# Hybrid encoder trunk: feature-major inputs, the first norm applied behind the projections, and the relative-bias rows copied in DRAM

## Chip, cores and metric

One core of one Trainium2 chip (trn2). The metric is the device time of one execution in microseconds (us), lower is better; a kernel's time is the median of its runs.

## The reference

A trunk of two layers over 272 tokens (16 meta tokens ahead of 256) with 1024 features, all in float32. In each layer an RMS norm, one input projection for four mixers in parallel (SSD, GLA, windowed attention "SWA", full attention "GQA"), one output projection, then a norm and a feed-forward block: SwiGLU in layer 0, eight experts with top 2 in layer 1.

```python
def _rmsnorm(x, w):
    xf = x * lax.rsqrt(jnp.mean(jnp.square(x), axis=-1, keepdims=True) + EPS)
    return xf * w

h = jnp.concatenate([meta, x], axis=1)
for i in range(2):
    u = _rmsnorm(h, norm_mix_w[i])
    (z, xbc, dt_raw, gq, gk, gv, gr, ga, sq, sk, sv, aq, ak, av) = jnp.split(u @ w_in[i], offs, axis=-1)
    y_ssd = _ssd_mixer(z, xbc, dt_raw, ...)
    y_gla = _gla_mixer(gq, gk, gv, gr, ga, ...)
    y_swa = _swa_mixer(sq, sk, sv, swa_sink[i], rel_bias)   # scores + rel_bias[bucket(key - query)]
    y_g2 = _gqa2d_mixer(aq, ak, av, ...)
    h = h + jnp.concatenate([y_ssd, y_gla, y_swa, y_g2], axis=-1) @ w_out[i]
    h = h + (_swiglu, _moe)[i](_rmsnorm(h, norm_ffn_w[i]), ...)
return _rmsnorm(h, final_norm_w)[:, 16:]
```

The bias of the windowed attention depends on key minus query alone: 543 distances times 4 heads, the same in both layers.

## The kernel before

The residual `hT` and the normed input `uT` lie feature-major: [128 features, 8 chunks, 272 tokens]. A float32 product is made of three float32r products (`mm3`, `proj_mm`): every operand is held as a high part, which ScalarE (ACT) casts (L144), and a low part, which VectorE (DVE), or for some tiles GpSimd (POOL), subtracts (L145). So each 1 MB weight tile `w` that SP loads (L140) gives two pairs of `wx` tiles of 128x1024. The pool `wa` has three buffers for the loaded tiles; a load waits in SP's queue until the splits of an earlier tile are done. SP issues in order: a load that waits holds all behind it. TensorE (PE) runs the products. Each engine's order is set ahead by the scheduler, which simulates a timeline from the program's order and a few hints (`high_priority`, `issue_after`).

**First norm.** `x` comes token-major. ACT squares it with row sums (L249 to L251), `rsx` becomes the inverse root, 24 transposes on PE give `hT` (L277), and 24 products with the diagonal matrices `dg` of the factors (in `normed`, L256 to L272) give the normed, transposed chunks `xn`, which ACT and DVE split into `uTh` and `uTl`. In layer 0 the projections thus need no factor: `evac` (L441) copies on ACT. In layer 1, `uT` comes without the factors, and `evac` multiplies by `rsB`, the factors on every partition, on DVE.

**Parameters.** 118 rows of parameters arrive by a dozen small loads and are transposed into the columns `colsP` (L294); others come through POOL's queue (L284 to L290).

**Projections of layer 0**, in PE's order: `dtga` (SSD steps and GLA gates), `gq`, `gk`, `gv`, the six `xbc` blocks of SSD, then those of the attentions, `z` and the gates, between mixer work.

**The relative bias** (`late_setup`, L298 to L334) is set up once, after GLA's front. `fb` [4 heads, 543] is the product of `rel_bias` with a one-hot matrix. It is written to DRAM 128 times per head, and read back skewed, with a row pitch one shorter than the row, so that partition q sees the distances of query q:

```python
scr = dr.tile([4, 128, RELW], F32, name='scr')
SP.dma_start(scr, fb[:, None, :].to_broadcast([4, 128, RELW]))
SP.dma_start(bias[j], bass.AP(tensor=scr.tensor, offset=scr.offset + o,
                              ap=[[RELW - 1, 128], [128 * RELW, 4], [1, L]]))
V.tensor_tensor(bias[j], bias[j], msk[:, j:j + 1, :].to_broadcast([128, 4, L]), op=ALU.add)
```

`bias` serves the windowed attention alone, whose scores come after SSD's and the full attention's first work. The SSD tiles spoken of below: `e` (L640, L699), masked decays times scores of the meta keys, and `y` (L118), its product with `x`.

Of the kernel before, what the change touches and what calls it, by code (L numbers as in the profile page):

```python
# [33 lines left out]
RELW = 543  # L34


def _consts():
# [30 lines left out]
    put('selP', np.arange(8)[:, None] % 4 == (p // 32)[None])  # L68
# [25 lines left out]
    ds = np.zeros((128, 256))  # L94
    for j in range(2):
        ds[:4, 128 * j:128 * j + 128] = 2 * j + (p // 64)[None] == np.arange(4)[:, None]
    masks = np.concatenate(m + [ds], axis=1).astype(np.float32)
# [13 lines left out]
def build(tc, A, out, off):  # L111
# [63 lines left out]
    colsP = cp.tile([128, 118], F32, name='colsP')  # L175
# [19 lines left out]
    def pow_rs(s_, o_, scale, eps):  # L195
        """o_ = (s_ * scale + eps) ** -0.5"""
# [17 lines left out]
    xt = [st.tile([128, D], F32, name=f'xt{j}') for j in range(2)]  # L214
    xm = st.tile([16, D], F32, name='xm')
    rows0 = st.tile([16, 128], F32, name='rows0')
    rows = st.tile([118, 128], F32, name='rows')
    SP = nc.sync
    SP.dma_start(xt[0], A['x'][0, 0:128, :])
    SP.dma_start(ident, A['cst'][:, 0:128])  # L220
    SP.dma_start(xm, A['meta_tokens'])
    SP.dma_start(xt[1], A['x'][0, 128:256, :])
    SP.dma_start(rows0, A['norm_mix_w'].rearrange('l (c p) -> (l c) p', p=128))
    win = load_win(0, UNITS[:0])
    SP.dma_start(rows[0:16], A['norm_mix_w'].rearrange('l (c p) -> (l c) p', p=128))
    SP.dma_start(rows[16:24], A['norm_ffn_w'][0].rearrange('(c p) -> c p', p=128))
    SP.dma_start(rows[24:84], A['ssd_conv_w'].rearrange('l k (c p) -> (l k c) p', p=128))
    SP.dma_start(rows[84:96], A['ssd_conv_b'].rearrange('l (c p) -> (l c) p', p=128))
    SP.dma_start(rows[96:100], A['ssd_norm_w'].rearrange('l (c p) -> (l c) p', p=128))
    SP.dma_start(rows[100:104], A['gla_gate_b'].rearrange('l d p -> (l d) p'))  # L230
    for i, nme in enumerate(('gla_norm_w', 'gqa_q_norm_w', 'gqa_k_norm_w')):
        SP.dma_start(rows[104 + 2 * i:106 + 2 * i].rearrange('l (r p) -> l r p', r=2),
                     A[nme][:, None, :].to_broadcast([2, 2, 64]))
# [11 lines left out]
    # first norm, token-major, then transposed  # L245
    junk = st.tile([128, D], F32, name='junk', bufs=2)
    ssx = st.tile([128, 3], F32, name='ssx')
    V.memset(ssx, 1.0)
    SC.activation(junk, xt[0], AF.Square, accum_out=ssx[:, 0:1])  # L249
    SC.activation(junk[:16], xm, AF.Square, accum_out=ssx[:16, 2:3])  # L250
    SC.activation(junk, xt[1], AF.Square, accum_out=ssx[:, 1:2])  # L251
    with tc.high_priority(100):
        rs0 = pow_rs(ssx, rsx, 1.0 / D, EPS)
    uT = [wx.tile([128, DC, L], F32R, name=n, tag=n) for n in ('uTh', 'uTl')]
# [3 lines left out]
    def normed():
        dg = st.tile([128, 3, 128], F32, name='dg')
        col0 = st.tile([128, 16], F32, name='col0')  # L260
        b = pp('cols')
        PE.transpose(b[:, :16], rows0, ident[:16, :16])
        V.tensor_copy(col0, b[:, :16])
        for i, (o, n) in enumerate(TOK):
            V.tensor_scalar(dg[:n, i, :n], ident[:n, :n], rsx[:n, i:i + 1], None, op0=ALU.mult)
        for c in range(DC):
            b = (bm if c % 2 == 0 else mb_)('xn')
            for i, ((o, n), src) in enumerate(zip(TOK, (xt[0], xt[1], xm))):
                last = mm(b[:, o:o + n], src[:n, c * 128:(c + 1) * 128], dg[:n, i, :n])
            un_[:] = [SC.activation(uT[0][:, c, :], b[:, :L], AF.Copy, scale=col0[:, c:c + 1]),  # L270
                      V.scalar_tensor_tensor(uT[1][:, c, :], b[:, :L], col0[:, c:c + 1], uT[0][:, c, :].bitcast(F32),
                                             op0=ALU.mult, op1=ALU.subtract), last]  # L272

    for c in range(DC):
        b = mb_('xT')
        for (o, n), src in zip(TOK, (xt[0], xt[1], xm)):
            PE.transpose(b[:, o:o + n], src[:n, c * 128:(c + 1) * 128], ident[:n, :n])  # L277
        (SC.copy if str(c) in '345' else V.tensor_copy)(hT[:, c, :], b[:, :L])
        if c == 8 - 1:
            with tc.high_priority(100):  # L280
                normed()

    with tc.issue_after(rs0.ins):
        GP.dma_start(dtb, A['ssd_dt_bias'].rearrange('l d h -> (d h) l'))  # L284
        GP.dma_start(acol, A['ssd_a_log'].rearrange('l d h -> (d h) l'))
        for l in range(2):
            for d in range(2):
                GP.dma_start(w2p[32 + 16 * d:48 + 16 * d, l, d, :], A['gla_gate_w2'][l, d])
        GP.dma_start(ds4, A['ssd_d'].rearrange('l h -> h l'))
        GP.dma_start(sink, A['swa_sink'].rearrange('l h -> (l h)')[None, :].to_broadcast([128, 8]))  # L290

    # parameter columns
    b = mb_('cols')
    PE.transpose(b[:, :118], rows, ident[:118, :118])  # L294
    V.tensor_copy(colsP, b[:, :118])
    sctx.close()

    def late_setup(st):  # L298
        V.tensor_copy(selH, K('sel8')[:8])
        V.tensor_copy(selP, K('selP')[:8])  # L300
        relb = st.tile([32, 4], F32, name='relb')
        SP.dma_start(relb, A['rel_bias'])
        oh = st.tile([128, 4 * L], F32, name='oh', tag='P', bufs=3)[:32, :RELW]
        SP.dma_start(oh, A['oh'])
        mskd = st.tile([128, 4 * L], F32, name='mskd', tag='P', bufs=3)[:, :3 * L + 256]
        SP.dma_start(mskd, A['masks'])
        msk = mskd[:, :3 * L].rearrange('p (a k) -> p a k', a=3)
        dsel = mskd[:4, 3 * L:].rearrange('p (a k) -> p a k', a=2)
        b = mb_('dsk')
        for j in range(2):  # L310
            mm(b[:, 2 * j:2 * j + 2], dsel[:, j, :], ds4)
        V.tensor_copy(dskip, b[:, :4].rearrange('p (j l) -> p j l', j=2))
        tmp4 = st.tile([128, 2, 4], F32, name='tmp4')
        V.tensor_tensor(tmp4, sink, K('hsel')[:, None, :].to_broadcast([128, 2, 4]), op=ALU.mult)
        V.tensor_reduce(sink4, tmp4, axis=AX.X, op=ALU.add)

        # T5 bias: row of all distances, then skewed through DRAM to [q, k]
        fb = st.tile([128, 4 * L], F32, name='fb', tag='P', bufs=3)[:4, :RELW]
        for a0, w in ((0, 272), (272, 271)):
            b = mb_('fb')  # L320
            mm(b[:4, :w], relb, oh[:, a0:a0 + w])
            SC.copy(fb[:, a0:a0 + w], b[:4, :w])
# [1362 lines left out]
```

## Time and profile before

| | us |
|---|---|
| runs (3) | 1667.57, 1668.33, 1671.43; median 1668.33 |
| span of the profiled execution, which is its own time | 1668.1 |
| PE busy | 1603.3 (96%) |
| DVE busy | 1270.2 (76%) |
| ACT busy | 998.1 (60%) |
| POOL busy | 77.6 (5%) |

The span is that of one execution under the profiler, 0.2 us below the median of the runs. Busy shares are means over the mixers (about the first 210 us and some 200 us of layer 1), the SwiGLU and the experts, which have different limits. PE is TensorE's matmuls, PEld its weight loads, SPq the queue of DMA issues on SP. PEclk is the granted share of TensorE's full clock of 2.4 GHz: 0.50 is its lower level, 1.2 GHz.

### The profile page before, as it was taken

The page shows a single profiled execution, that of the slowest core. Times are in us where ns is not written, and L with a number is a line of the kernel's source. Part 1 is how long each engine was busy: PE and PEld are TensorE (multiplying, and loading weights), DVE is VectorE, ACT ScalarE, POOL GpSimd, SP SyncE. Part 2 cuts the span into 40 slices and gives each one's busy share as a digit, 9 for nine tenths or more (in the row PEclk, how much of TensorE's full clock was granted, in tenths as well). Part 3 has the DMA queues.
Part 4 walks back from the last instruction along what each step waited for, and adds up shares of the span by engine and source line. Part 5 has one row for each costly group of instructions (what it writes and reads, how often), then busy time and mean ns, then how long its engine had stood idle before and what let it go on. Part 6 is the DMA issues. An engine that isn't in the chain of part 4 may idle for free.

```text
span 1668.1 us, 22234 instructions
## 1 busy us (share of the span) xinstructions
PE 1603.3 (96%) x8904; PEld 1359.8 (82%) x8904; DVE 1270.2 (76%) x1389; ACT 998.1 (60%) x1024; POOL 77.6 (5%) x73
## 2 busy tenths in 40 slices
PE   8965999999999999999999999999999999999996
PEld 7854579999998879888888888888888888888875
DVE  4814446565568667888988988988988988888986
ACT  4512345444444545767767767767767767676764
POOL 3122000000003200000000000000000000000000
PEclk9976679999999999999999999999999999999999
DMA  6424016555433348899999999999999999999980
GB/s 206 135 23 135 1 50 217 170 172 173 129 106 118 127 158 307 321 349 353 355 349 353 356 349 353 355 349 354 355 351 353 353 352 353 348 332 352 360 310 27
DMA packets 219158, 428.24 MB, mean 257 GB/s; under 512 B 8121, under 2 KB 70137, under 8 KB 218921
## 3 DMA queue, kind: packets, MB, share of 16 engines
q1 hardware_dynamic: 218793, 426.73, 72.6%
q8 instruction: 71, 1.16, 0.3%
q14 instruction: 38, 0.31, 0.1%
q0 software_dynamic: 256, 0.04, 0.0%
HBM read 424.58 MB, written 2.16 MB: 256 GB/s over the span
## 4 chain that ended last, share of the span: by engine, by line
PE 87%; DVE 5%; DMA 5%; issue 1%; ACT 1%; SPq 0%; POOL 0%; POOLq 0%; ACTq 0%; DVEq 0%
PE dn L1543 12%; PE eg L1511 6%; PE eg L1507 6%; PE eg L1508 6%; PE dn L1546 6%; PE eu L1511 6%; PE eu L1507 6%; PE eu L1508 6%; DMA scr<-fb 3%; PE wo L1197 2%; PE at L119 2%; PE xe L119 2%; PE ehT L1525 1%; PE u L163 1%; PE at L118 1%
## 5 line engine op out<-in xcount | busy, mean ns | idle before, releaser
L145 DVE TENSOR_TENSOR wl<-w,wh 128x2048 fp32r<-128x2048 f32 (+1 forms) x343 | 767.2, 2245 | 110.6 <-ACT wh L144 109.2
L144 ACT CAST wh<-w 128x2048 fp32r<-128x2048 f32 (+1 forms) x343 | 638.6, 1875 | 226.4 <-PE dn L1546 97.7
L1543 PE MATMUL dn<-wh,ehh 128*128 128x512 f32 x448 | 176.5, 397 | 0.0
L1546 PE MATMUL dn<-wh,ehl 128*128 128x512 f32 x448 | 175.5, 394 | 0.8 <-DVE ehl L145 0.8
L1507 PE MATMUL eu<-wh,xe 128*128 128x512 f32 x448 | 176.2, 393 | 0.0
L1507 PE MATMUL eg<-wh,xe 128*128 128x512 f32 x448 | 175.7, 392 | 0.0
L1508 PE MATMUL eg<-wh,xe 128*128 128x512 f32 x448 | 175.3, 391 | 0.0
L1508 PE MATMUL eu<-wh,xe 128*128 128x512 f32 x448 | 174.6, 390 | 0.0
L144 ACT CAST wx<-w 128x1024 fp32r<-128x1024 f32 (+1 forms) x86 | 87.5, 1026 | 97.9 <-DMA w<-in_w_in 53.0
L1543 PE MATMUL dn<-wl,ehh 128*128 128x512 f32 x448 | 144.7, 398 | 0.1
L1511 PE MATMUL eg<-wl,xe 128*128 128x512 f32 x448 | 125.6, 402 | 0.0
L1511 PE MATMUL eu<-wl,xe 128*128 128x512 f32 x448 | 121.9, 391 | 0.5 <-DVE wl L145 0.5
L145 DVE TENSOR_TENSOR wx<-w,wx 128x1024 fp32r<-128x1024 f32 (+2 forms) x75 | 88.9, 1192 | 38.6 <-ACT wx L144 38.2
L1546 PEld LDWEIGHTS dn<-wh,ehl 128*128 128x128 f32 x448 | 84.2, 188 | 20.7 <-DVE ehl L145 1.3
L1543 PEld LDWEIGHTS dn<-wh,ehh 128*128 128x128 f32 x448 | 84.2, 188 | 20.1
L1507 PEld LDWEIGHTS eg<-wh,xe 128*128 128x128 f32 x448 | 84.1, 188 | 19.3
L1543 PEld LDWEIGHTS dn<-wl,ehh 128*128 128x128 f32 x448 | 83.4, 188 | 20.1 <-DVE wl L145 1.0
L1508 PEld LDWEIGHTS eg<-wh,xe 128*128 128x128 f32 x448 | 84.1, 188 | 18.8
L1511 PEld LDWEIGHTS eu<-wl,xe 128*128 128x128 f32 x448 | 84.0, 188 | 18.8 <-DVE wl L145 1.3
L1507 PEld LDWEIGHTS eu<-wh,xe 128*128 128x128 f32 x448 | 84.2, 188 | 17.9 <-ACT wh L144 0.6
L1508 PEld LDWEIGHTS eu<-wh,xe 128*128 128x128 f32 x448 | 84.2, 188 | 16.9
L1511 PEld LDWEIGHTS eg<-wl,xe 128*128 128x128 f32 x448 | 80.2, 189 | 14.7
(533 smaller groups left out, 2792.9 us busy)
## 6 DMA issues: line engine op xcount, KB each, us to landing
w<-in_moe_w_gate SPq DMA_DIRECT2D x112, 1024.0 KB
w<-in_moe_w_up SPq DMA_DIRECT2D x112, 1024.0 KB
w<-in_moe_w_down SPq DMA_DIRECT2D x112, 1024.0 KB
w<-in_w_in SPq DMA_DIRECT2D x20, 1024.0 KB
w<-in_ffn_w_gate SPq DMA_DIRECT2D x11, 1024.0 KB
w<-in_ffn_w_up SPq DMA_DIRECT2D x11, 1024.0 KB
w<-in_w_out SPq DMA_DIRECT2D x8, 1024.0 KB
w<-in_ffn_w_down SPq DMA_DIRECT2D x8, 1024.0 KB
```

Source lines behind the costliest of these rows:

```text
L118: return PE.matmul(o, a, b, start=start, stop=stop, skip_group_check=True)
L119: return PE.matmul(o, a, b, start=start, stop=stop)
L144: a = SC.copy(hi, src)
L145: return a, (eng or V).tensor_tensor(lo, src, hi.bitcast(F32), op=ALU.subtract)
L163: PE.matmul(o, a[1], b[0], start=False, stop=stop)
L1197: PE.matmul(o, a, mixT[0][:, 4 * kh + k, q0:], start=(p_ == k == 0), stop=(p_ == 1 and k == 3))
L1507: PE.matmul(b, xe[0][:, k, :], w[0][:, kk, :], start=(k == 0), stop=False)
L1508: PE.matmul(b, xe[1][:, k, :], w[0][:, kk, :], start=False, stop=False)
L1511: PE.matmul(b, xe[0][:, k, :], w[1][:, kk, :], start=False, stop=(k == DC - 1))
L1525: PE.transpose(b[:, 128 * i:128 * i + 128], sg[:, 128 * i:128 * i + 128], ident)
L1543: PE.matmul(dn[n], eh[0][:, i, :], o, start=(fb == 0 and i == 0 and p_ == 0), stop=(last and i == 3 and p_ == 1))
L1546: PE.matmul(dn[n], eh[1][:, i, :], o, start=False, stop=False)
```

## The change

- **Inputs laid out by the host**: `hT0` is the residual, feature-major; `par` [128, 136] has all parameter columns, with the SSD steps', decays', skips' and sinks' values; `w2p` the gate weights with the selector `selP`. The token-major loads, the transposes, `normed`, the dozen row loads and the POOL loads go.
- **First norm at the evacuations**: `uT` is the split of `hT` times the norm's weight, without the factors. POOL squares the eight chunks, PE sums them with 24 one-column products, and `rsx` follows. `rsB` is made in layer 0 too, so `evac`, the gates and the `sq` evacuations multiply by it on DVE, and `projv` scales three blocks on ACT.
- **Bias rows**: `fb` is made right after the sums; POOL's queue writes it to DRAM once (`scr0`) and copies it there 128 times (`scr`), with the queries outermost.

```diff
-    SP.dma_start(xt[0], A['x'][0, 0:128, :])
...
-    SP.dma_start(rows[110:118], A['norm_ffn_w'][1].rearrange('(c p) -> c p', p=128))
+    SP.dma_start(par, A['par'])
+    for c in range(0, DC, 2):
+        SP.dma_start(hT[:, c:c + 2], A['hT0'][:, c:c + 2])
     SP.dma_start(ident, A['cst'][:, 0:128])
...
+    GP.dma_start(relb, A['rel_bias'])
+    GP.dma_start(oh, A['oh'])
...
+    bs = mb_('stat')
     for c in range(DC):
...
+        un_[:] = [SC.activation(uT[0][:, c, :], hT[:, c, :], AF.Copy, scale=col(c)),
+                  V.scalar_tensor_tensor(uT[1][:, c, :], hT[:, c, :], col(c), uT[0][:, c, :].bitcast(F32),
+                                         op0=ALU.mult, op1=ALU.subtract)]
+        sq = st.tile([128, L], F32, name='sq0', bufs=4)
+        GP.tensor_tensor(sq, hT[:, c, :], hT[:, c, :], op=ALU.mult)
+        with tc.manual_schedule(engines={mybir.EngineType.PE}):
+            for i, (o, n) in enumerate(TOK):
+                last = mm(bs[:n, i:i + 1], sq[:, o:o + n], ones[:, 0:1], start=(c == 0 and i == 0), stop=(c == DC - 1), skip=True)
...
+    scr0 = dr.tile([4, RELW], F32, name='scr0')
+    scr = dr.tile([128, 4 * RELW], F32, name='scr')
+    for a0, w in ((0, 272), (272, 271)):
+        b = mb_('fb')
+        with tc.issue_after(last.ins):
+            mm(b[:4, :w], relb, oh[:, a0:a0 + w])
+        SC.copy(fb[:, a0:a0 + w], b[:4, :w])
     with tc.issue_after(rs0.ins):
...
+        GP.dma_start(scr0, fb)
+        GP.dma_start(scr, scr0.rearrange('h r -> (h r)')[None, :].to_broadcast([128, 4 * RELW]))
...
-        scr = dr.tile([4, 128, RELW], F32, name='scr')
-        SP.dma_start(scr, fb[:, None, :].to_broadcast([4, 128, RELW]))
         for j, o in ((0, REL0 - 16), (1, REL0 - 144)):
             SP.dma_start(bias[j], bass.AP(tensor=scr.tensor, offset=scr.offset + o,
-                                          ap=[[RELW - 1, 128], [128 * RELW, 4], [1, L]]))
+                                          ap=[[4 * RELW - 1, 128], [RELW, 4], [1, L]]))
...
-        if rooted:
-            rsB = rs_rows(mp)
+        rsB = rs_rows(mp if l else wk)
...
-                if a == 2 and rsB is not None:
+                if a == 2:
                     evac(sq_[:, a, :], b)
+                elif l == 0:
+                    V.scalar_tensor_tensor(sq_[:, a, :], b[:, :L], 0.125, rsB, op0=ALU.mult, op1=ALU.mult)
```

The program's order shifts with it at three places. SP's queue in layer 0, from the mask load to the first output weights, before (`bias_75` and `bias_76` are the two query blocks, `bias_77` the meta queries, `w` a weight tile):

```order
L306 DMA mskd<-in_masks 128x1072
L140 DMA w<-in_w_in 128x8x256 x8
L324 DMA scr<-fb 512x1x543
L326 DMA bias_75<-scr 128x4x272
L326 DMA bias_76<-scr 128x4x272
L329 DMA bias_77<-scr 32x272 x3
L140 DMA w<-in_w_in 128x8x256
L329 DMA bias_77<-scr 32x272
L140 DMA w<-in_w_out 128x4x512 x4
```

and now:

```order
L223 DMA w2p<-in_w2p 64x512
L137 DMA w<-in_w_in 128x8x256 x4
L271 DMA mskd<-in_masks 128x816
L275 DMA bias_75<-scr 128x4x272
L275 DMA bias_76<-scr 128x4x272
L278 DMA bias_77<-scr 32x272 x4
L137 DMA w<-in_w_in 128x8x256 x6
L137 DMA w<-in_w_out 128x4x512 x4
```

The write of `scr` has left SP's queue, and the bias loads have moved ahead: six `w_in` loads stand behind them now, where one did.

DVE around the first bias add, before (`w_963` are the SSD decays of all heads):

```order
L674 TENSOR_REDUCE m_985<-t_984 128x6
L664 SCALAR_TENSOR_TENSOR w_963<-cst,tk,w_963 128x128
L333 TENSOR_TENSOR bias_75<-bias_75,mskd 128x1088
L758 TENSOR_TENSOR w_963<-w_963,cbs 128x128 x2
L710 TENSOR_SCALAR w_1116<-cst,m_985 128x16
L664 SCALAR_TENSOR_TENSOR w_963<-cst,tk,w_963 128x128 x2
L333 TENSOR_TENSOR bias_76<-bias_76,mskd 128x1088
```

and now (`s_290` are the SSD steps, `xg`, `gn` and `en` GLA's decays):

```order
L142 TENSOR_TENSOR s3l<-s_290,s3h 8x544
L485 TENSOR_TENSOR xg<-gb 128x256
L282 TENSOR_TENSOR bias_75<-bias_75,mskd 128x1088
L142 TENSOR_TENSOR wx<-w,wx 128x1024
L794 TENSOR_TENSOR gn<-eb,gq 128x544
L795 TENSOR_TENSOR en<-en,gk 128x544
L791 TENSOR_TENSOR xg<-xg,gk 128x272
L282 TENSOR_TENSOR bias_76<-bias_76,mskd 128x1088
L792 TENSOR_TENSOR xg<-xg,gk 128x256
L283 TENSOR_TENSOR bias_77<-bias_77,mskd 128x272
```

The bias adds have moved from the end of SSD's decays to GLA's front, ahead of weight splits and of GLA's products with `gq` and `gk`; L485 is the former L537.

POOL now, from the last squares on (`scr_230` is `scr0`):

```order
L243 TENSOR_TENSOR sq_207<-hT 128x272
L243 TENSOR_TENSOR sq_217<-hT 128x272
L251 TENSOR_TENSOR rsx<-rsx,nhalf 128x3
L262 DMA scr_230<-fb 4x543
L142 TENSOR_TENSOR wx<-w,wx 128x1024 x2
L263 DMA scr<-scr_230 128x2172
L1054 TENSOR_SCALAR rw_1261<-cst,par 128x128
```

The two weight splits, which POOL had before as well, stand between the two DMAs of the bias rows.

## Rows read from the trace of the kernel before

**Rows 1.** The page: its head, and the busy time of the engines.
```profile
span 1668.1 us, 22234 instructions
...
PE 1603.3 (96%) x8904; PEld 1359.8 (82%) x8904; DVE 1270.2 (76%) x1389; ACT 998.1 (60%) x1024; POOL 77.6 (5%) x73
```

**Rows 2.** Waits of PE: us in total, times, longest.
```profile
PE y L118 <- DVE e L699: 35.9, 1, 35.9
```

**Rows 3.** Chain of waits from 84 to 146 us: start, us, what.
```profile
86.62 45.28 DMA scr<-fb
...
131.93 0.37 SPq L326
...
134.59 6.50 DMA w<-in_w_in
...
142.23 1.28 ACT L640
...
144.03 0.49 DVE e L699
```

**Rows 4.** Waits of SP's queue and DVE; ACT's timeline (start, us, [idle before, releaser]).
```profile
SPq L326 <- DMA scr<-fb: 44.5, 1, 44.5
...
DVE bias L333 <- DMA bias<-scr: 39.0, 1, 39.0
...
141.17 1.04 ACT L144 CAST wx<-w 128x1024 fp32r<-128x1024 f32 x1 [38.79 <-DMA w<-in_w_in]
```

**Rows 5.** Stretches: busy us (instructions) of each engine, clock, DMA share, GB/s.
```profile
40.00:60.00 20.00, 20.00 (x216) 19.27 (x214) 19.83 (x48) 15.13 (x32) 0.00 (x0) 1.00 0.58 189
...
84.00:88.00 4.00, 4.00 (x17) 2.85 (x16) 0.15 (x1) 1.53 (x4) 0.00 (x0) 0.50 0.00 0
...
104.00:108.00 4.00, 4.00 (x33) 3.79 (x32) 0.00 (x0) 0.00 (x0) 0.00 (x0) 1.00 0.23 26
...
136.00:140.00 4.00, 0.00 (x0) 0.00 (x0) 4.00 (x11) 0.00 (x0) 0.00 (x0) 0.50 1.11 333
...
148.00:152.00 4.00, 4.00 (x20) 3.94 (x20) 2.18 (x10) 0.31 (x1) 0.82 (x1) 0.50 0.00 0
152.00:156.00 4.00, 4.00 (x22) 4.00 (x23) 0.20 (x4) 0.72 (x2) 3.61 (x2) 0.62 0.00 0
```
The busy times stand in the order PE, PEld, DVE, ACT, POOL.

**Rows 6.** DMA issues: queue, count, KB each, median us to landing.
```profile
scr<-fb SPq DMA_DIRECT2D x1, 1086.0 KB
...
w2p<-in_gla_gate_w POOLq DMA_DIRECT2D x4, 8.0 KB, 5.7
```

**Rows 7.** Timeline of PE in the first 30 us: start, us, what, [idle before].
```profile
7.02 0.47 PE L277 MATMUL xT<-ident,xt 128*128 128x128 f32 x1 [1.21 <-DMA xt<-in_x]
...
22.05 0.59 PE L424 MATMUL dtga<-uTh,wx 128*128 128x272 f32 x1
...
29.43 2.02 PE L427 MATMUL dtga<-uTh,wx 128*128 128x272 f32 x8
```

**Rows 8.** Timelines of POOL and of DVE, 33 to 44 us.
```profile
33.52 4.78 POOL L145 TENSOR_TENSOR wx<-w,wx 128x1024 fp32r<-128x1024 f32 x2 [2.08 <-ACT wx L144]
...
36.52 2.37 DVE L517 SCALAR_TENSOR_TENSOR gn<-xg 128x544 f32<-128x544 f32 x1 [0.47 <-ACT xg L514]
...
42.95 0.69 DVE L527 SCALAR_TENSOR_TENSOR xg<-xg,gn 128x544 f32<-128x544 f32 x1
```

**Rows 9.** Timeline of DVE: the GLA subtraction, and the bias adds.
```profile
48.79 0.41 DVE L537 TENSOR_TENSOR xg<-gb 128x256 f32<-128x256 f32 x1
...
135.83 1.29 DVE L333 TENSOR_TENSOR bias<-bias,mskd 128x1088 f32<-128x1088 f32 x1 [39.01 <-DMA bias<-scr]
...
141.41 0.44 DVE L334 TENSOR_TENSOR bias<-bias,mskd 128x272 f32<-128x272 f32 x1
```

**Rows 10.** Instructions of line L445, layer 1's evacuations: ns least, median, most.
```profile
L445 DVE TENSOR_TENSOR xpad<-xbc,rsBs x6: 426/430/442, 500.2 to 524.2; 128x272 f32<-128x272 f32 x6
```

More of the change, by code (lines that the diff above doesn't have):

```diff
@@ L93, in _consts @@
     m.append(np.where(np.abs(rel) <= 128, 0.0, NEG))
[L94 to L97, printed above, removed]
+    masks = np.concatenate(m, axis=1).astype(np.float32)
     rel = np.arange(RELW) - REL0
@@ L174, in build @@
     bias4 = cp.tile([128, L], F32, name='bias4')
-    colsP = cp.tile([128, 118], F32, name='colsP')
+    par = cp.tile([128, PARW], F32, name='par')
+    colsP = par[:, 0:118]
+    dtb, acol = par[:8, 118:120], par[:8, 120:122]
+    dskip = par[:, 122:126].rearrange('p (j l) -> p j l', j=2)
+    sink = par[:, 126:134].rearrange('p (l h) -> p l h', l=2)
+    sink4 = par[:, 134:136]
     w2p = cp.tile([64, 2, 2, 128], F32, name='w2p')
@@ L213, in build @@
     st = sctx.enter_context(tc.tile_pool(name='st', bufs=1, side='right', reuse_waits='tile'))
[L214 to L217, printed above, removed]
     SP = nc.sync
-    SP.dma_start(xt[0], A['x'][0, 0:128, :])
+    relb = st.tile([32, 4], F32, name='relb')
+    oh = st.tile([32, RELW], F32, name='oh')
+    fb = st.tile([4, RELW], F32, name='fb')
+    SP.dma_start(par, A['par'])
+    for c in range(0, DC, 2):
+        SP.dma_start(hT[:, c:c + 2], A['hT0'][:, c:c + 2])
     SP.dma_start(ident, A['cst'][:, 0:128])
-    SP.dma_start(xm, A['meta_tokens'])
-    SP.dma_start(xt[1], A['x'][0, 128:256, :])
-    SP.dma_start(rows0, A['norm_mix_w'].rearrange('l (c p) -> (l c) p', p=128))
     win = load_win(0, UNITS[:0])
[L225 to L233, printed above, removed]
-    SP.dma_start(rows[110:118], A['norm_ffn_w'][1].rearrange('(c p) -> c p', p=128))
     win.update(load_win(0, UNITS[0:3]))
+    GP.dma_start(relb, A['rel_bias'])
+    GP.dma_start(oh, A['oh'])
     SP.dma_start(cst, A['cst'][:, 128:])
+    SP.dma_start(w2p, A['w2p'])
     win.update(load_win(0, UNITS[3:]))
@@ L243, in build @@
         V.memset(azm[d], 0.0)
[L246 to L254, printed above, removed]
@@ L256, in build @@
-    un_ = []
[L258 to L272, printed above, removed]
@@ L274, in build @@
-    for c in range(DC):
[L275 to L281, printed above, removed]
-    with tc.issue_after(rs0.ins):
[L284 to L290, printed above, removed]
@@ L293, in build, with pair_wx @@
-    b = mb_('cols')
-    PE.transpose(b[:, :118], rows, ident[:118, :118])
-    V.tensor_copy(colsP, b[:, :118])
+    def pair_wx(n):
+        return wx.tile([128, DC, L], F32R, name=n, tag=n)
+    uT = [pair_wx(n) for n in ('uTh', 'uTl')]
+    un_ = []
+    bs = mb_('stat')
+    for c in range(DC):
+        un_[:] = [SC.activation(uT[0][:, c, :], hT[:, c, :], AF.Copy, scale=col(c)),
[6 more added lines that the diff above has]
+                last = mm(bs[:n, i:i + 1], sq[:, o:o + n], ones[:, 0:1], start=(c == 0 and i == 0), stop=(c == DC - 1), skip=True)
@@ L299, in late_setup @@
         V.tensor_copy(selH, K('sel8')[:8])
[L300 to L305, printed above, removed]
-        SP.dma_start(mskd, A['masks'])
[L307 to L322, printed above, removed]
-        scr = dr.tile([4, 128, RELW], F32, name='scr')
-        SP.dma_start(scr, fb[:, None, :].to_broadcast([4, 128, RELW]))
+        V.tensor_copy(selP, w2p[0:8, 0, 0, :])
+        mskd = st.tile([128, 4 * L], F32, name='mskd', tag='P', bufs=3)[:, :3 * L]
+        SP.dma_start(mskd, A['masks'])
+        msk = mskd.rearrange('p (a k) -> p a k', a=3)
         for j, o in ((0, REL0 - 16), (1, REL0 - 144)):
             SP.dma_start(bias[j], bass.AP(tensor=scr.tensor, offset=scr.offset + o,
-                                          ap=[[RELW - 1, 128], [128 * RELW, 4], [1, L]]))
+                                          ap=[[4 * RELW - 1, 128], [RELW, 4], [1, L]]))
         for h in range(4):
             SP.dma_start(bias4[32 * h:32 * h + 32],
-                         bass.AP(tensor=scr.tensor, offset=scr.offset + h * 128 * RELW + REL0,
-                                 ap=[[RELW - 1, 32], [1, L]]))
+                         bass.AP(tensor=scr.tensor, offset=scr.offset + h * RELW + REL0,
+                                 ap=[[4 * RELW - 1, 32], [1, L]]))
         for j in range(2):
@@ L390, in put @@
             if not mixT:
-                mixT.extend(wx.tile([128, DC, L], F32R, name=n, tag=t) if rsB is None else pair(n, t)
+                mixT.extend(pair(n, t) if l else wx.tile([128, DC, L], F32R, name=n, tag=t)
                             for n, t in (('mixh', 'uTh'), ('mixl', 'uTl')))
@@ L1664, in build, with _laid @@
     ctx.close()
[L1667 to L1669 removed]
+_INS = ['rel_bias', 'w_in', 'w_out', 'ffn_w_gate', 'ffn_w_up', 'ffn_w_down', 'moe_router',
         'moe_w_gate', 'moe_w_up', 'moe_w_down', 'final_norm_w']
+def _laid(g):
+    h = np.concatenate([g('meta_tokens'), g('x')[0]], axis=0)
+    rows = [g('norm_mix_w').reshape(16, 128), g('norm_ffn_w')[0].reshape(8, 128), g('ssd_conv_w').reshape(60, 128),
+            g('ssd_conv_b').reshape(12, 128), g('ssd_norm_w').reshape(4, 128), g('gla_gate_b').reshape(4, 128),
+            np.tile(g('gla_norm_w'), (1, 2)), np.tile(g('gqa_q_norm_w'), (1, 2)), np.tile(g('gqa_k_norm_w'), (1, 2)),
+            g('norm_ffn_w')[1].reshape(8, 128)]
+    par = np.zeros((128, PARW), np.float32)
+    par[:, 0:118] = np.concatenate(rows, axis=0).T
+    par[:8, 118:120] = g('ssd_dt_bias').reshape(2, 8).T
+    par[:8, 120:122] = g('ssd_a_log').reshape(2, 8).T
+    par[:, 122:126] = np.repeat(g('ssd_d').reshape(2, 2, 2).transpose(2, 1, 0), 64, axis=0).reshape(128, 4)
+    par[:, 126:134] = np.broadcast_to(g('swa_sink').reshape(1, 8), (128, 8))
+    par[:, 134:136] = np.repeat(g('swa_sink').T, 32, axis=0)
+    w2p = np.zeros((4, 16, 2, 2, 128), np.float32)
+    w2p[0, :8, 0, 0] = np.arange(8)[:, None] % 4 == (np.arange(128) // 32)[None]
+    for d in range(2):
+        w2p[2 + d, :, :, d] = g('gla_gate_w2')[:, d].transpose(1, 0, 2)
+    return {'hT0': h.T.reshape(DC, 128, L).transpose(1, 0, 2), 'par': par, 'w2p': w2p.reshape(64, 2, 2, 128)}
 def kernel(**inputs):
@@ L1675 @@
     arrays = {n: np.ascontiguousarray(np.asarray(inputs[n])) for n in _INS}
-    arrays.update(cst=first, masks=masks, oh=oh, moec=moe)
+    laid = _laid(lambda n: np.asarray(inputs[n]))
+    arrays.update({n: np.ascontiguousarray(a) for n, a in laid.items()}, cst=first, masks=masks, oh=oh, moec=moe)
     nc = bacc.Bacc("TRN2", target_bir_lowering=False, num_devices=1)
```

21 lines of the change are left out of this document (8 added, 13 removed).

## The prediction, made before the changed kernel was run

> **What bounds the kernel now.** I read the page first. TensorE (PE) is busy for 1603.3 of 1668.1 us [rows 1]: over most of the span there is nothing to gain except from fewer or faster matmuls, and the change leaves those after layer 0's mixers as they are. So I looked for the places where PE waits. The list of PE's waits has one large entry, 35.9 us in one piece, before the SSD product `y` of layer 0; it names a DVE instruction on tile `e` as the releaser [rows 2]. That name is only the last link. The chain of waits from 84 to 146 us shows what stands behind it: the write `scr<-fb` to DRAM takes 45.28 us, the bias loads follow at 131.93, and behind them on the same queue the last `w_in` load of the layer is issued only at 134.59; then come ScalarE's (ACT's) table load at 142.23, and `e` on DVE at 144.03 [rows 3]. The waits of the other engines say the same: SP's queue waits 44.5 us for `scr`, DVE 39.0 us for the bias, ACT 38.8 us for the `w_in` load [rows 4]. Three engines stand behind one transfer. The stretches show why it is slow and what it costs besides: between 104 and 108 us only 0.23 of the 16 DMA engines are busy and 26 GB/s move, where the loads at 136 to 140 us reach 333 GB/s; and when PE resumes, it runs at a granted clock of 0.50, the lower level (1.2 GHz), with 20 matmuls in 4 us, where at full clock 33 fit [rows 5].
>
> **What the change removes: the stall.** The new `scr` is filled from DRAM with the 128 queries outermost, on GpSimd's (POOL's) queue, at the start. If it has landed before anyone needs it, the stall goes. What is late next? DVE waited 39.0 us until 135.83 [rows 4, 9], so without the wait it comes to this place at 96.8; its work from there to `e` (135.83 to 144.03, less two bias adds of 1.29 and one of 0.44 us [rows 9]) takes about 5.2 us. ACT needs a cast of 1.04 us [rows 4] and the 1.80 us from table load to `e` [rows 3]. Both are done by about 106 us, while PE, whose wait of 35.9 us ended at 144.57, has its own work until 108.7. So the whole **35.9 us** goes, with 2 to 3 us of cover left; evacuations now on DVE could eat into that, and the front below pays for them.
>
> **The clock.** Half clock lasts from 144.57 to about 155 (a mean of 0.62 from 152 to 156 is three quarters of that window at 0.50), 10.5 us at 20 matmuls per 4 us. At 33 per 4 us, as between 104 and 108 where PE is busy throughout [rows 5], the same work takes 6.4 us. I take **4.1 us**; the ends are 0, if PE has another gap ahead of this work, and half of 10.5, 5.2.
>
> **The new copy.** No transfer of DRAM to DRAM is in the trace; its price must be bounded. The old one moved 1086 KB [rows 6] in 45.28 us with 0.23 x 16 = 3.7 engines busy [rows 5], 6.5 GB/s for each. With the same bytes on 16 engines at that pace it takes 1086 KB / 104 GB/s = 10.4 us; at the 333 GB/s of plain loads, 3.3 us; on four engines, the 45 us of now; on two, 84; on one, 168. I take 10 us, because the outermost size 128 is that of the plain loads, which reach 333. The Trainium skill, "DMA: Bandwidth & Descriptors", section Rules for kernel authors, says that an outermost dimension smaller than 16 confines a DMA to that many engines; the old write with its four heads outermost, at a share of 0.23, agrees, and by that rule the new one has all 16.
>
> How late may it land? `hT` arrives about when the second token tile does now (7.0 us [rows 7]). POOL then squares eight tiles of 272 columns; two of its 1024-column operations take 4.78 us [rows 8], so one square takes some 0.63 and all eight 5 us. The first `dtga` matmul, now at 22.05, can start at about 14, since 24 transposes and 24 diagonal products no longer stand before it. The row `scr0` goes out at about 15 and takes 5 to 6 us, as the small POOL transfers do (5.7 us [rows 6]). On POOL's queue two weight splits now stand ahead of `scr`; the second waits for `dtga`'s 24 matmuls (2.02 us for 8 [rows 7], so 6 us) and a cast: `scr` is issued at about 24. It is needed by DVE's first bias add, which the change moves far forward, behind the GLA decay subtraction that now runs at 48.79 [rows 9]; 8 us of earlier front and two splits fewer ahead of it (1.2 each), less evacuations, bring that to about 39. A bias load takes 135.83 - 131.93 = 3.9 us. So 39 - 3.9 - 24 = **11 us of copy are free**; every further one is DVE's, with six `w_in` loads behind it on SP. At 10 us the wait costs 0.
>
> **The front.** Removed: transposes, diagonal products, three ACT squares of 1024 columns, the small parameter loads. That starts the projections 22.05 - 14 = 8 us earlier. Given back: DVE's three bias adds (3.0 us [rows 9]) now stand in the stretch from 40 to 60 us, where DVE is busy 19.83 of 20 us [rows 5], and the `gq`, `gk` and six `xpad` evacuations become DVE products with the norm's factors, 8 x 0.43 = 3.4 us (layer 1 has the same form at 430 ns [rows 10]). ACT loses as many copies but is not the limit there. The later products for `gx` and `sq` fall where DVE waits. Net 8.0 - 3.0 - 3.4 = **1.6 us**. Its ends: all 8 us (DVE finds slack after all), and -5 (rival 2). The 24 one-column statistic matmuls, the rows of `fb` and the factors' broadcast hide beside the `uT` casts and loads; without that cover they cost at most 2 to 3 us, within these ends. Parameters that came through POOL's queue and through transposes come in one load, earlier than their users: nothing.
>
> **Sum.** 1668.1 - 35.9 - 4.1 - 1.6 = **1626.5 us**. The profiled span is 0.2 us below the median of the runs, so I don't correct for it. After the mixers of layer 0 the order of the instructions is the same, and PE limits it, so the shift is carried to the end.
>
> **The rivals.**
> 1. *The copy is the stall again, in another place (slower).* The copy's source is a single row read 128 times, and its queue is POOL's, of which the trace shows only small transfers; if it ran on few engines, DVE would wait at the first bias add, and the splits behind it and SP's six `w_in` loads would wait too, so PE would starve from about 40 us. From 11 us on each microsecond counts: at 45 us 1626.5 + 34 = 1660; slower than now from 58 us (47 past the free 11); on two engines, 84 us, about 1699. For it: the 3.7 engines of the old write. Against it: its four heads outermost, which the new one hasn't.
> 2. *The front gives nothing.* POOL squares while DVE subtracts `uTl`, each with two operands in SBUF. The trace has such a pair: DVE's `gn` takes 2.37 us while POOL splits weights, where an operation of the same shape takes 0.69 without POOL [rows 8]. If all eight subtractions are held by squares, the front loses eight times 0.63 us, 5 us: 1626.5 + 5 = 1631.5, at worst 1633 with the gain gone as well. The Trainium skill, "GPSIMD Engine Reference", section Key points, says that POOL shares its SBUF interfaces with DVE and contends with DVE instructions that have two SBUF inputs. The pair of rows agrees.
> 3. *The front keeps all of its 8 us*: 1620, and to 1612 if the half clock between 84 and 88 us (17 matmuls in 4 us [rows 5]) shrinks as well, for which nothing in the change speaks directly.
> 4. *Something else holds `e`*: the stall is only partly gone because evacuations on DVE or the last `w_in` load use up the 2 to 3 us of cover. 10 us of it would give 1636.
> 5. *The copy does not spread as written* and takes 20 to 58 us: 1636 to 1673.
>
> **How the numbers follow.** The forecast (copy within 15 us, the sum within 6 us) gets 0.58; rival 2 0.12; rival 3 0.12; rival 4 0.05; rival 5 0.08; rival 1 beyond 58 us 0.05. The range 1612 to 1645 holds the forecast, rivals 2 to 4 and the start of rival 5, about 0.88, which leaves room for misjudged terms. A measurement of this kernel tells about 0.3% (5 us) from no change: faster, below 1663.3, has 0.91 (the forecast and rivals 2 to 4 with 0.87, and half of rival 5), within 0.3% 0.04 (its other half), slower 0.05 (rival 1).
>
> **What would show it.** Right: no large wait of PE before `y`; `scr` lands before 40 us with a DMA share near 1 for some 10 us; DVE's first bias add waits little; the clock stays at 1.00 past 108 us; `dtga` starts at about 14. Wrong: a wait of DVE at the first bias add for `bias<-scr` of over 5 us with a low DMA share (rivals 1, 5); `uTl` subtractions of over 1 us (rival 2); another releaser before `y` (rival 4).

## The result, and the profile after

The changed kernel takes 1614.34 us (median of 4 runs, 1603.14 to 1623.58) against 1667.95 us before; the ratio is 0.9666, 95% interval 0.961 to 0.9722. Measured again later, beside experiments 4 and 6, it took 1624.59 us (6 runs, 1614.52 to 1631.08) against 1670.33, ratio 0.9733 (0.9693 to 0.9774). The runs of this kernel spread by more than one per cent; what moves with it is the granted clock, as the last section shows. Ratios are of fast runs alone, which leaves out one run of experiment 5. The forecast was 1626.5 us in a range of 1612 to 1645.

The page of the changed kernel, its head and busy times:

```profile
span 1614.0 us, 22170 instructions
...
PE 1577.4 (98%) x8880; PEld 1341.2 (83%) x8880; DVE 1275.0 (79%) x1399; ACT 989.0 (61%) x1003; POOL 80.9 (5%) x77
```

PE's busy share is 98% where it was 96% [rows 1]. The waits of PE (us in total, times, longest), longest first, have lost the entry of 35.9 us [rows 2]; what is longest now is the start of the kernel and a short gap in the front:

```profile
PE stat L115 <- POOL sq L243: 4.8, 1, 4.8
PE gate L116 <- issue: 3.4, 1, 3.4
```

The chain of waits of the first 120 us (start, us, what) shows the copy where 45.28 us stood [rows 3]:

```profile
23.30 2.30 POOL wx L142
25.60 8.44 DMA scr<-scr
34.05 6.12 DMA bias<-scr
```

It is issued at 25.60, behind the two POOL splits, takes 8.44 us, with a weight load and the mask load in flight beside it, and the bias is in SBUF at 40.2. In the trace up to 15 of the copy's packets are under way at once, where the old write has at most 4. The timeline of DVE (start, us, what, [idle before, releaser]) shows the first bias add right then:

```profile
40.19 1.29 DVE L282 TENSOR_TENSOR bias<-bias,mskd 128x1088 f32<-128x1088 f32 x1 [2.41 <-DMA bias<-scr]
```

DVE waits 2.41 us there, where it waited 39.01 [rows 9]. On PE's timeline:

```profile
4.82 8.71 PE L115 MATMUL stat<-ones,sq 128*128 128x1 f32 x48 [4.82 <-POOL sq L243]
...
15.36 0.60 PE L373 MATMUL dtga<-uTh,wx 128*128 128x272 f32 x1
...
19.09 1.16 PE L376 MATMUL dtga<-uTh,wx 128*128 128x272 f32 x8
...
99.43 1.13 PE L115 MATMUL y<-e,x 128*128 128x256 f32 x4
```

PE sums the squares until 13.5 us, makes `fb`, and starts `dtga` at 15.36 (22.05 before [rows 7]); `y` comes at 99.43, with no idle time ahead of it (144.57 before). The stretches after `y` (busy us of PE, PEld, DVE, ACT, POOL, then clock, DMA share, GB/s) hold a surprise:

```profile
84.00:88.00 4.00, 4.00 (x28) 3.44 (x28) 2.37 (x6) 1.49 (x3) 4.00 (x5) 1.00 0.01 4
...
100.00:104.00 4.00, 4.00 (x21) 3.64 (x19) 2.79 (x7) 0.31 (x1) 1.50 (x1) 0.61 0.00 0
104.00:108.00 4.00, 4.00 (x22) 3.97 (x22) 0.85 (x6) 0.00 (x0) 2.36 (x2) 0.53 0.02 4
```

The half clock that stood at 84 to 88 us before [rows 5] is gone, but after `y` the clock falls to its lower level all the same, with PE busy throughout.

To see where the 54.1 us between the two profiled executions went, every execution is divided at the first matmul of four products on PE's timeline: `y` and `wo` (output projection) of layer 0, `dtga` and `wo` of layer 1. In brackets is the half-clock time: over stretches of 2 us, PE's busy time times twice the clock missing from 1. Experiments are explained below.

| us (half clock) | to `y` | `y` to `wo` | `wo` to layer 1 | layer 1's mixers | rest | span |
|---|---|---|---|---|---|---|
| before | 144.6 (10.2) | 93.0 (61.6) | 235.1 (3.4) | 138.1 (20.4) | 1057.4 | 1668.1 |
| after | 99.4 (3.4) | 86.9 (47.7) | 233.5 (0.0) | 136.4 (10.2) | 1057.8 | 1614.0 |
| after, again | 98.8 (3.4) | 86.8 (47.1) | 233.7 (0.5) | 136.5 (13.6) | 1056.9 | 1612.7 |
| norm and layout alone | 130.2 (0.0) | 88.9 (54.7) | 237.8 (6.5) | 144.7 (34.5) | 1058.1 | 1659.7 |
| the same, again | 130.5 (0.0) | 91.7 (60.8) | 238.1 (6.0) | 148.0 (42.1) | 1057.3 | 1665.5 |
| bias part alone | 111.2 (6.8) | 86.9 (49.8) | 236.4 (4.6) | 148.1 (41.8) | 1058.0 | 1640.6 |
| heads first | 108.4 (7.5) | 85.4 (44.3) | 233.4 (0.0) | 139.8 (16.7) | 1057.8 | 1624.8 |
| from SBUF, heads first | 136.5 (9.5) | 87.8 (49.4) | 234.2 (1.8) | 144.0 (27.1) | 1054.8 | 1657.4 |
| squares on ACT | 101.1 (6.7) | 88.5 (51.1) | 233.4 (0.0) | 136.3 (10.2) | 1057.7 | 1617.1 |
| early factors | 96.9 (5.6) | 96.7 (59.9) | 231.2 (1.5) | 148.1 (43.5) | 1057.0 | 1629.8 |
| the same, again | 93.8 (0.0) | 83.9 (30.6) | 232.0 (3.4) | 148.3 (43.7) | 1057.9 | 1616.0 |
| early factors, late adds | 98.0 (6.6) | 97.3 (61.3) | 230.5 (0.0) | 132.7 (6.8) | 1057.2 | 1615.6 |

From before to after: 45.2 us up to `y`, 6.1 behind it in layer 0's mixers, 1.6 in `wo` and SwiGLU, 1.7 in layer 1's mixers; the experts are unchanged. The half clock fell by 34.3 us in all; at the 20 and 33 matmuls per 4 us that the prediction took, one microsecond of it costs 0.39 us, so by this estimate 13 of the 54 us are clock. A row is one execution. Those of "after, again", "from SBUF" and "late adds" are each the fastest run of their kernel: the other five runs of the changed kernel beside them, 1619.59 to 1631.08 us at mean clocks of 0.963 to 0.972, left no trace, so which of these stages made them longer is not known.

### The profile page after: what moved, and what is told of

Its sections match the earlier page's. It is cut to its first block, busy times and chain, and to the rows that moved or that the text cites. A ratio compares the mean times of both kernels' runs of the same rounds, so it can differ in the third digit from the quotient of the medians.

```text
span 1614.0 us, 22170 instructions
## 1 busy us (share of the span) xinstructions
PE 1577.4 (98%) x8880; PEld 1341.2 (83%) x8880; DVE 1275.0 (79%) x1399; ACT 989.0 (61%) x1003; POOL 80.9 (5%) x77
## 4 chain that ended last, share of the span: by engine, by line
PE 87%; DVE 6%; DMA 4%; issue 1%; ACT 1%; POOL 0%; POOLq 0%; SPq 0%; ACTq 0%; DVEq 0%
PE dn L1493 12%; PE eg L1461 6%; PE eg L1457 6%; PE dn L1496 6%; PE eg L1458 6%; PE eu L1458 6%; PE eu L1457 6%; PE eu L1461 6%; PE wo L1147 2%; PE xe L116 2%; PE at L116 2%; DMA w<-in_w_in 2%; PE ehT L1475 1%; PE u L160 1%; PE g L158 1%
## 5 line engine op out<-in xcount | busy, mean ns | idle before, releaser
L1493 PE MATMUL dn<-wl,ehh 128*128 128x512 f32 x448 | 144.7, 398 | 0.2
L141 ACT CAST wx<-w 128x1024 fp32r<-128x1024 f32 (+2 forms) x86 | 87.8, 1027 | 78.9 <-DMA w<-in_w_in 26.8
L142 DVE TENSOR_TENSOR wx<-w,wx 128x1024 fp32r<-128x1024 f32 (+2 forms) x75 | 88.9, 1194 | 43.5 <-ACT wx L141 43.3
```

The costliest lines, as they stand in the source:

```text
L141: a = SC.copy(hi, src)
L142: return a, (eng or V).tensor_tensor(lo, src, hi.bitcast(F32), op=ALU.subtract)
L1493: PE.matmul(dn[n], eh[0][:, i, :], o, start=(fb == 0 and i == 0 and p_ == 0), stop=(last and i == 3 and p_ == 1))
```

## The experiments

**1. The bias part alone.** The kernel before, with the rows made early and copied on POOL's queue:

```diff
+    GP.dma_start(relb, A['rel_bias'])
+    GP.dma_start(oh, A['oh'])
...
+    with tc.issue_after(rs0.ins):
+        GP.dma_start(scr0, fb)
+        GP.dma_start(scr, scr0.rearrange('h r -> (h r)')[None, :].to_broadcast([128, 4 * RELW]))
...
-        scr = dr.tile([4, 128, RELW], F32, name='scr')
-        SP.dma_start(scr, fb[:, None, :].to_broadcast([4, 128, RELW]))
```

> The kernel before with the bias part of the change alone (rows made early, copied in DRAM on POOL's queue with the queries outermost, bias adds in front). Theory: the parts add, and this one carries the stall: PE's wait of 35.9 us before y is gone, the front is no earlier (three bias adds now in it), the half clock after y comes anyway: 1628 to 1636 us. Rival: the 16 us that the change gained beyond the stall are also the stall's doing (the clock it lowered, what piled up behind it): 1613 to 1620 us.

Measured: 1641.6 us, ratio 0.9815 (0.9782 to 0.9848). Neither range holds it. Its DMA issues (queue, count, KB, us to landing) show the copy as fast as in the full change:

```profile
scr<-scr POOLq DMA_DIRECT2D x1, 1086.0 KB, 7.7
```

The wait before `y` is gone and `y` comes 33.4 us earlier, 35.9 less a front that is 2.5 us later (three bias adds in it). The half clock right after `y`, which the theory kept, is gone as well. A stretch just behind `y` (111.2):

```profile
112.00:116.00 4.00, 4.00 (x33) 3.73 (x32) 3.01 (x11) 0.31 (x1) 1.93 (x2) 1.00 0.01 4
```

Before, the clock was 0.50 there, with 20 matmuls in 4 us [rows 5]. Up to layer 1 this part gains 38.2 us: 434.5 (the sum of the first three columns) against 472.7. Then layer 1's mixers take 148.1 us where before took 138.1, with twice the half clock. That was in neither theory.

**2. Norm and layout alone.** The changed kernel with the old bias rows:

```diff
-        GP.dma_start(scr0, fb)
-        GP.dma_start(scr, scr0.rearrange('h r -> (h r)')[None, :].to_broadcast([128, 4 * RELW]))
...
+        scr = dr.tile([4, 128, RELW], F32, name='scr')
+        SP.dma_start(scr, fb[:, None, :].to_broadcast([4, 128, RELW]))
```

> The changed kernel with the bias part taken back (rows made late, written by SP with the heads outermost). Theory: the layout and norm part alone moves the front forward by some 9 us, the write of scr starts that much earlier, and the stall of some 36 us before y stays: 1655 to 1662 us. Rival: the front's gain is swallowed by the stall or by the evacuations on DVE: 1665 to 1669 us.

Measured: 1662.34 us, ratio 0.9947 (0.9927 to 0.9968), just past the theory's range. The waits of PE:

```profile
PE y L115 <- DVE e L645: 38.1, 1, 38.1
```

and the chain, the same write as before:

```profile
72.49 45.27 DMA scr<-fb
```

PE reaches the end of `av` at 92.1 us (130.2 less 38.1) instead of 108.7: this part alone gains 16.6 us up to there. The write starts only 14.1 us earlier (86.62 to 72.49), so the stall grows by 2.2, and `y` gains 14.3. Layer 1's mixers then take 6.6 us more, with 14.1 us more of half clock. The two parts gain 8 and 29 us by their medians, 37 in sum, less than the change as a whole: 54 us in its first runs and 46 in its second, which stood beside experiments 4 and 6 and not beside these. Up to `wo` of layer 0 the parts gain 18.5 (15.4 in the second execution) and 39.5, 58.0 in sum, and the change 51.2. There the parts overlap a little (the bias adds cost the front something). Behind it the sign turns: in layer 1's mixers the parts lose 6.6 and 10.0 us, and the change gains 1.7.

**3. Heads first.** The changed kernel, the destination of the DRAM copy as [4, 128, 543] again:

```diff
-    scr = dr.tile([128, 4 * RELW], F32, name='scr')
+    scr = dr.tile([4, 128, RELW], F32, name='scr')
...
-        GP.dma_start(scr, scr0.rearrange('h r -> (h r)')[None, :].to_broadcast([128, 4 * RELW]))
+        GP.dma_start(scr, scr0[:, None, :].to_broadcast([4, 128, RELW]))
```

> The changed kernel, with the DRAM copy's destination laid out heads first again (512 rows of 2172 bytes, outermost size 4), same queue and same source. Theory: the layout made the copy fast; with heads first it takes about 45 us with a quarter of the engines, DVE waits some 35 us at the first bias add, and six w_in loads wait behind it: 1645 to 1652 us. Rival: the queue and the DRAM source made it fast: 8 to 12 us for the copy, 1612 to 1620 us.

Measured: 1624.49 us, ratio 0.9725 (0.9678 to 0.9771): neither. Its DMA issue, the wait of DVE, and a stretch in which hardly anything else is loaded:

```profile
scr<-scr POOLq DMA_DIRECT2D x1, 1086.0 KB, 18.9
```
```profile
DVE bias L282 <- DMA bias<-scr: 10.4, 1, 10.4
```
```profile
34.00:36.00 2.00, 2.00 (x19) 2.00 (x18) 2.00 (x5) 0.92 (x2) 0.00 (x0) 1.00 0.25 100
```

A share of 0.25 is four engines, as the layout says, but they move 100 GB/s (96 of them the copy's, 24 for each engine; the rest is the end of the mask load), where the old write moved 26 with as many [rows 5]. So the layout was one limit and not the only one. The delay is passed on about one for one: DVE waits 8.0 us longer than in the changed kernel, and `y` is 9.0 us later.

**4. From SBUF, heads first.** The old write from the new place, on POOL's queue:

```diff
-        GP.dma_start(scr0, fb)
-        GP.dma_start(scr, scr0.rearrange('h r -> (h r)')[None, :].to_broadcast([128, 4 * RELW]))
+        GP.dma_start(scr, fb[:, None, :].to_broadcast([4, 128, RELW]))
```

> The changed kernel with the 128 copies written straight from SBUF (no scr0), heads first, on POOL's queue: the old write from the new place. Theory: the source is the second limit; four partitions feed four engines at 6.5 GB/s each, so it takes about 45 us where the heads-first copy from DRAM took 18.9; issued at about 17 us it lands at about 62, DVE waits some 28 us at the first bias add: 1638 to 1650 us. Rival: SP's queue made the old write slow: about 19 us here too, landing at 36 to 38, 1612 to 1620 us.

Measured: 1668.48 us, ratio 0.9982 (0.9954 to 1.0011), no gain at all, and above both ranges. The same three views:

```profile
scr<-fb POOLq DMA_DIRECT2D x1, 1086.0 KB, 48.5
```
```profile
DVE bias L280 <- DMA bias<-scr: 37.8, 1, 37.8
```
```profile
40.00:44.00 4.00, 0.00 (x0) 0.00 (x0) 0.00 (x0) 0.00 (x0) 0.00 (x0) 0.73 0.25 30
```

With the source in four SBUF partitions the four engines move 30 GB/s, of which the copy's are 24 (the rest is the mask load), on POOL's queue as on SP's (26 [rows 5]). So the source is the second limit, and the queue is none. It is not SBUF as such that is slow: in the changed kernel the last store, `out<-res`, reads 128 partitions at 379 GB/s with nearly all engines:

```profile
1608.00:1610.00 2.00, 0.00 (x0) 0.00 (x0) 0.00 (x0) 0.00 (x0) 0.00 (x0) 0.50 0.96 379
```

That is 25 GB/s for each engine, as from DRAM. Not run was the write from SBUF with the queries outermost: whether the four partitions limit each engine or all engines together, and so whether the step through `scr0` was needed, is open. The early stall costs what the prediction's first rival said up to `y`: 136.5, 37.1 us later than in the changed kernel for 35.4 us more of waiting. The theory's time was too low because DVE waits 37.8 us where 28 were expected, and layer 1's mixers have 27.1 us of half clock.

**5. Squares on ACT.**

```diff
-        GP.tensor_tensor(sq, hT[:, c, :], hT[:, c, :], op=ALU.mult)
+        SC.activation(sq, hT[:, c, :], AF.Square)
```

> The changed kernel with the eight squares on ACT instead of POOL. Theory: POOL's squares and DVE's subtractions hold each other up (0.76 us where 0.50 us stood), but the product dtga waits for the sums and the bias rows, so the time stays: uTl at 0.50 us each, total 1610 to 1618 us. Rival: the contention is on the path and costs what it takes: 1608 to 1611 us, dtga 2 us or more earlier.

Measured: 1619.07 us, ratio 0.9658 (0.9614 to 0.9702), a microsecond above the theory's range. The line of the subtractions (ns least, median, most; first and last start), of the changed kernel and then of this one:

```profile
L240 DVE SCALAR_TENSOR_TENSOR uTl<-hT,par,uTh x8: 500/872/877, 4.6 to 9.8; 128x272 fp32r<-128x272 f32 x8
```
```profile
L240 DVE SCALAR_TENSOR_TENSOR uTl<-hT,par,uTh x8: 494/502/503, 4.6 to 9.6; 128x272 fp32r<-128x272 f32 x8
```

POOL's squares do lengthen DVE's subtractions, from 502 to 872 ns, but the last one starts at nearly the same time (9.8 and 9.6 us), since without POOL's squares DVE waits for ACT's casts instead. `dtga` starts at 15.5 instead of 15.4: in both kernels PE itself holds it, for the sums of the squares take PE 8.71 us and end at 13.5 and 13.6, when the last subtraction is long done (10.7 us in the changed kernel). The contention is real and hidden.

**6. Early factors, and late adds.** Two tries at a faster version. The first puts ACT's copy of `rsBs` (`rsc[0]`) ahead of two casts of weights, those of the second `gv` block and of the first `xbc` block:

```diff
+                if l == 0 and f0 in (1416, 256):
+                    after.enter_context(tc.issue_after(rsc[0].ins))
                 split(hl[0], hl[1], t[:, :, o:o + 128], eng)
```

> The changed kernel with ACT's copy of the factors (rsBs) ahead of two weight casts, which held it although its product was ready 4 us earlier. Theory: PE's 3.4 us wait before the gate product goes, but the bias loads, which land at about 40 us, then hold DVE's first bias add longer, so y comes only 0 to 2 us earlier: 1611 to 1616 us. Rival: the whole 3.4 us carries through, y at 96 us: 1609 to 1612 us.

The second also puts the bias adds behind the last `xpad` evacuation:

```diff
+        with tc.issue_after(done):
             for j in range(2):
                 V.tensor_tensor(bias[j], bias[j], msk[:, j:j + 1, :].to_broadcast([128, 4, L]), op=ALU.add)
```

> The factors' copy early, and the three bias adds behind the last SSD evacuation on DVE. Theory: neither the factors nor the bias rows hold DVE now; gate 3.4 us earlier and no wait at the bias: y at 93 to 96 us, 1606 to 1611 us. Rival: the scheduler's other order in layer 1 meets a longer stretch at half clock there, as in the two single parts (5 to 8 us): y at 93 to 96 us and yet 1613 to 1620 us.

The changed kernel ran beside them again:

> The changed kernel again, as the measure for the others on the same chip: 1608 to 1620 us, half clock in layer 1's mixers about 10 us as in its first profile if it belongs to the program, anything between 10 and 40 us if it falls by chance.

It took 1624.59 us, ratio 0.9733 (0.9693 to 0.9774), above what was expected, with the half clock of layer 1 as in its first profile. The first try took 1631.16 us, ratio 0.9769 (0.9734 to 0.9804), and the second 1625.92, ratio 0.975 (0.9707 to 0.9793), both above every range that was given. In the first the gate's wait went, and a new one of the same length took its place, in PE's waits:

```profile
PE v L375 <- DVE gk L398: 3.4, 1, 3.4
```

`y` comes 2.5 and 1.4 us earlier in these profiles (5.6 in the first's second execution, experiment 7). Behind it the way to `wo` is 9.8 and 10.4 us longer; the half clock, 12.2 and 13.6 us more there, makes some 5 of each by the 0.39, and the rest is not explained. Neither version beats the changed kernel that ran beside it.

**7. Two kernels again.** The first executions left open whether the half clock falls by chance.

> The kernel with the early factors a second time, for its profile alone. If the stretches at half clock belong to the program (the order of its instructions), layer 1's mixers have some 43 us of half clock and take 148 us again, as in its first profile; if they fall by chance, anything between 7 and 43 us.

> The norm and layout part alone a second time, for its profile. If the half clock belongs to the program: some 34 us of it in layer 1's mixers and 145 us for them, as before; by chance: anything between 7 and 43 us.

In layer 1's mixers the early factors have 43.5 and 43.7 us of half clock in two executions, norm and layout alone 34.5 and 42.1, the changed kernel 10.2 and 13.6. Two executions of a kernel lie within 8 us of each other there and the kernels up to 33 apart, which speaks for the program as far as two executions of each can. Between `y` and `wo` of layer 0 the early factors have 59.9 and 30.6 us of it, and 96.7 and 83.9 us of time: there it differs from one execution to the next.

## Why the prediction held, and where it did not

**The stall: right.** The 35.9 us are gone, for the reason given: without the bias part the wait stays (38.1 us, experiment 2), with the bias part alone it goes (experiment 1), and nothing else was late at `y`.

**The copy: right in time, wrong in its bounds.** 10 us were taken, 8.4 measured. Issue was put at 24 (25.6), DVE's arrival at 39 (37.8), the wait at 0 (2.4, mostly because a bias load took 6.1 us where 3.9 stood before). But "on four engines, the 45 us of now" was wrong for a copy from DRAM: four engines took 18.9 (experiment 3). The prediction read the pace per engine of the old write, 6.5 GB/s, as a property of the transfer to DRAM; it belonged to the source in four partitions (experiment 4). So the 10.4 us that came out of this pace on 16 engines lie near the 8.4 in part by luck. The Trainium skill's rule ("DMA: Bandwidth & Descriptors", Rules for kernel authors) that a small outermost dimension confines a DMA to at most as many engines agrees with the shares of 0.25. With the source in DRAM this is worth 18.9 against 8.4 us, less than half of the way from 45 to 8.

**The front: the step that starts the projections 8 us earlier was mis-sized, and so was what is given back.** `dtga` started 6.7 us earlier. The sums and the products for `fb`, which were to hide beside casts and loads, did not: PE is busy with them until 15.4 us, while `uTl` was done at 10.7 and the first weight splits on DVE at 13.1, so they cost some 2 us. But the last group of `dtga` came 10.3 us earlier (29.43 to 19.09), because diagonal products had stood between its matmuls as well. In experiment 2, without the bias part, this group starts at 17.5 and the last `xbc` group at 56.5 instead of 67.9: 11.9 us gained and 11.4 kept, so the evacuations on DVE, priced at 3.4, cost next to nothing. In the changed kernel that group starts at 65.1: the bias part costs the front 8.5 us, not 3.0. PE's own rows tell where. `dtga`'s last group is 1.6 us later (`fb`). PE waits 3.4 us before `gate`, because ACT copies the factors `rsBs` at 25.2 us, behind a weight cast, and in experiment 2 at 21.3, ahead of it. It waits 1.5 us before `kdT` for a product that DVE makes behind the first bias add, and 0.8 for an `xpad` evacuation. And 3.4 us at half clock cost 1.3. Less the 0.5 us that PE waits in experiment 2, this is 8.1 of the 8.5. The largest piece is thus an order on ACT that no term of the sum had. The net at that place, 2.9 us, lies near the forecast of 1.6 by two errors of opposite sign. From there to `y` another 6.4 us came in (9.2 without the stall, in all), of which the half clock that stood at 80 to 91 us before, 10.2 us at 0.39, accounts for 4.0.

**The clock: the one term was half right, and all else of the clock was left out.** The prediction put the half clock after `y` down to the stall and counted 4.1 us for it. In the 12 us after `y` the three traces with the stall (before, and experiment 2 twice) have 10.1 to 12.0 us of half clock. Of the nine traces without it six have none, experiment 1 among them, and three have 6.8: the changed kernel twice, and the late adds. In these three the clock falls only 1.5 to 2.0 us behind the start of `y`, with PE busy throughout (0.61 and 0.53 at 100 to 108 us in the changed kernel), so it is not left over from a wait; why it falls there is not shown. In the changed kernel the term thus gave about 1.4 us (3.7 us less of half clock) of its 4.1.

What failed is the step that counted no other clock. Between `y` and `wo` the half clock lasts 47 us in the changed kernel, 55 and 61 with the stall (experiment 2), 60 and 31 without it (experiments 6 and 7): what it is there doesn't follow from the stall. The 13 us that the clock gave in the profiled pair are 9 more than counted, of the 12.5 between 1626.5 and 1614; most of the other 3 are the front's. In the second set of runs the mean clocks were lower (0.963 to 0.975, against 0.969 to 0.984) and the time was 1624.6: that this lies within 2 us of the forecast is in part luck.

**"After the mixers of layer 0 the order of the instructions is the same": wrong for layer 1's mixers.** The scheduler simulates the whole program, and a shift in layer 0 changes the order in which ACT's, DVE's and PE's work of layer 1's mixers is laid out, though its code is the same. The kernels with the changed kernel's order there (heads first and squares on ACT, but for two neighbours on DVE) have 10 to 17 us of half clock, those with other orders 7 to 44, and the stage takes 133 to 148 us. But the order in this stage doesn't settle it alone. The two kernels of experiment 6 run the same instructions in the same order there on PE, ACT, DVE and POOL, and yet the early factors have 43.5 and 43.7 us of half clock, and with the late adds it is 6.8; the stage takes 148 and 133 us. In both the clock falls 107 to 108 us behind `dtga`, and stays low for 37.5 us in the one and for 3.4 in the other. The same ten microseconds of both executions, the early factors first (the stage starts at 424.8 and 425.8):

```profile
548.00:558.00 10.00, 10.00 (x29) 5.51 (x28) 5.32 (x15) 3.52 (x9) 0.59 (x2) 0.50 0.00 0
```
```profile
548.00:558.00 10.00, 9.90 (x66) 7.76 (x65) 7.42 (x24) 4.51 (x14) 1.44 (x3) 1.00 0.01 2
```

What decides between them is open.

**The rivals.** The first (copy slow, slower kernel) did not happen, but its mechanism was priced right up to `y`: a microsecond of waiting for the copy cost about one (experiments 3 and 4). The copy and the bias load came 2.4 us later than DVE, where the prediction left a microsecond to spare. The second (POOL against DVE) happened without cost (experiment 5). The rule of the Trainium skill ("GPSIMD Engine Reference", Key points), that POOL contends with DVE instructions of two SBUF inputs, agrees with the 502 and 872 ns. The third, the front keeping its gain with the half clock at 84 us gone too, comes closest to what the first profile shows: 1612 to 1620, at a chance of 0.12. The changed kernel's own runs reach from there to the forecast.

## What to carry to other kernels

The broadcast through DRAM had two limits here: how many DMA engines its outermost dimension gave, and how fast four partitions could be read. A first small write of the distinct rows and a copy in DRAM with a large outermost dimension removed both (45 to 8 us). The long wait on a chain of three engines was worth its full length because the next-latest work was far enough ahead; price that distance, and count the clock's return behind it as a range that includes nothing. In a kernel that a scheduler lays out, compare before and after stage by stage, with the clock beside each stage, before crediting or blaming a part of the change: here the parts together seemed to gain 8 to 16 us less than the whole, and most of the difference arose in a stage whose code none of them touches.

## What was not expected of the hardware

Four DMA engines moved 96 GB/s from DRAM to DRAM (experiment 3) and 24 to 26 GB/s from four SBUF partitions to DRAM, whichever queue issued them (experiment 4, and the kernel before). The granted clock fell to its lower level with PE busy throughout, and with the same order of instructions it stayed there for 37.5 us in one kernel and 3.4 in another. The time of one program goes with the granted clock of the execution: the changed kernel took 1603.14 us at a mean clock of 0.984 and 1623.58 at 0.969, 1.4 us for each 0.001, about the 0.39 us per microsecond of half clock read from the stretches (0.015 x 2 x 1614 = 48 us of it, 20.4 us of time, 0.42 for each).
